# Three more output-projection steps by seven products, and another order of steps in the last three groups

## The chip, the core and the metric

The kernel runs on one core of a Trainium2 chip. The metric is the device time of one launch in microseconds; lower is better. The time before is 1044.01 us, the median of three runs that lie between 1043.68 and 1044.53.

## The reference, cut to what matters

One layer of a trunk: an RMS norm, a chunked gated linear attention with its output projection, a residual, another RMS norm and a squared-ReLU MLP, and a last RMS norm, for 256 tokens of width 2048 in float32. The change lives in the line of the output projection, `@ w_out`, a product of 256 x 2048 by 2048 x 2048.

```python
def _gla_mixer(h, w_in, w_gate_up, b_gate, o_norm, w_out):
    ...
    o = o.transpose(1, 0, 3, 2, 4).reshape(bsz, seq, GLA_VAL_WIDTH).astype(h.dtype)
    return (o * jax.nn.silu(r)) @ w_out
...
        h = h + _gla_mixer(_rmsnorm(h, gla_norm[j]), gla_w_in[j], gla_w_gate_up[j],
                           gla_b_gate[j], gla_o_norm[j], gla_w_out[j])
        h = h + _sq_relu_mlp(_rmsnorm(h, mlp_norm[i]), mlp_w_up[i], mlp_w_down[i])
    return _rmsnorm(h, final_norm)
```

## The kernel before

**Precision.** Every float32 operand is split into a rounded part (`hi`) and the rest (`lo`). A product is three matmuls: hi by hi, lo by hi, hi by lo. ScalarE makes `hi` by a copy (L118) and VectorE makes `lo` by a subtraction (L131, L165, L763). Split weights live in slots, `slots()`, five for `hi` and five for `lo`; a slot is free again when the last matmul that reads it is done. Raw weights come by DMA into six `raw` tiles.

**The stages.** The input projections come first, then attention, whose result `on` is gated; then the output projection (`out_group`, about 287 to 375 us), the up projection and the down projection of the MLP, and the last norm. TensorE's order is written out by hand: `then_mm` puts each block of matmuls behind the block before it. ScalarE's copies keep their order too (`copy_hi`). VectorE's order is less bound: each sum follows the split of its own step, and the split of the sums follows the split of the step after.

**A group and its steps.** The projection goes in four groups of 512 output columns. A group has eight steps, one for each pair `kp` of 128-row blocks of `w_out`, in an order given as a list. A step loads a 256 x 512 piece of weights. There are two ways to take it.

- A plain step: `lo` of all 1024 columns (two blocks of 512), and 24 matmuls of 256 columns.
- A step by sums: the 2 x 2 blocks of weights and activations are multiplied with seven products instead of eight, by sums and differences of blocks, 21 matmuls. One of the sums of weights is made by the DMA itself: the piece comes in two loads on the SP queue, and a third load on GpSimd's queue adds a block to one that has landed (L734). VectorE splits 768 columns (L131), makes two more sums in place (`weight_sums`, L597 and L598), and when ScalarE has copied those, splits them as well (1024 columns, L763, a second slot). This second half (`pending`) is multiplied behind the next step's products. Two PSUM banks hold sums over all the steps by sums of a group, `sums_banks`. When the last of these steps is done, ScalarE copies the two banks out (L769, L770), VectorE combines them (L771 to L774), and adds them to the group's two ordinary banks into `h` (L777).

The sums of activations, the *forms*, are made once, when `on` is transposed: `turn` transposes eight 128 x 128 blocks on TensorE (L620), and for a pair in `FORMED` calls `turn_pair`, which scales two blocks, makes the sums on VectorE (L610), and splits all eight blocks (L611 on ScalarE, L612 on VectorE). Other pairs get two plain scaled splits (L633 on ScalarE, L634 on VectorE for each of two row blocks).

**What goes on between steps.** `out_group` takes a table of calls to be made behind given steps. In the first group the last two turns of `on` stand behind the second step. In the other three, behind the second step stands the turn of the `h` of the group before (for the up projection), behind the fifth its squares (`ssq_h`, L782). Behind the fourth step `begin_out` copies the old `h` of the next group into its banks (L677).

The pairs by sums are 0, 1 and 7 in every group, so twelve steps of 32. Their order is 3, 0, 2, 1, 4, 7, 5, 6, in which the steps by sums are the second, the fourth and the sixth.

Of the kernel before, what the change touches and what calls it, by code (L numbers as in the profile page):

```python
# [33 lines left out]
T = 256  # L34
# [12 lines left out]
G = 1024  # L47
# [12 lines left out]
OFF = 48  # L60
# [8 lines left out]
def tile_gla_mlp(ctx, tc, x, xt, cols, w_vg, w_in, w_gate, w_out, w_up, w_down, final_norm, out):  # L69
# [19 lines left out]
    def aux_bank():  # L89
        aux_free.rotate(-1)  # L90
        return psum_bank(aux_free[-1], "aux")
# [151 lines left out]
    g2 = lambda kt: colt[:, KT + kt : KT + kt + 1]  # L243
# [88 lines left out]
    h = const.tile([P, NT, D], F32, name="h")  # L332
# [244 lines left out]
    oth = otl = None  # L577
# [13 lines left out]
    def form_sums(f, tt):  # L591
        tt(f[:, S3], f[:, A21], f[:, A11], ALU.subtract)
        tt(f[:, S2 : S1 + 1], f[:, A22 : A22 + 1].to_broadcast([P, 2, P]), f[:, 0::7], ALU.add)
        tt(f[:, S4], f[:, A12], f[:, S2], ALU.subtract)
# [2 lines left out]
        nc.vector.tensor_tensor(u[:, 2], u[:, 0], u[:, 2], op=ALU.subtract)  # L597
        return nc.vector.tensor_tensor(u[:, 1::2], u[:, 1::2], u[:, 2:3].to_broadcast([P, 2, T]), op=ALU.subtract)  # L598

    FORMED = (0, 1, 7)  # L600
    in_forms = lambda a: a.rearrange("p (f s) -> p f s", f=8)
    raw_forms = [in_forms(some[:, 4:6].rearrange("p a b -> p (a b)")), in_forms(mid.tile([P, G], F32, tag="db", name="form"))]

    def turn_pair(kp, bank, gain, to):

        raw_form = raw_forms[kp == 1]
        for i in range(2):
            s = bank[:, i * T : (i + 1) * T].rearrange("p (t s) -> p t s", t=NT)
            nc.scalar.activation(raw_form[:, A12 + 1 - i :: 2], s, AF.Copy, scale=gain(2 * kp + i))
        form_sums(raw_form, lambda o, x, y, op: nc.vector.tensor_tensor(o, x, y, op=op))  # L610
        nc.scalar.copy(to[0], raw_form)  # L611
        nc.vector.tensor_tensor(to[1], raw_form, to[0].bitcast(F32), op=ALU.subtract)  # L612

    def turn(src, row, gain, q, forms_of=None, banks=None):

        bs = banks or [aux_bank(), aux_bank()]
        for i in range(4):
            kt, b, o = 4 * q + i, bs[i // 2], i % 2 * T
            for t in range(NT):
                newest[0] = nc.tensor.matmul(  # L620
                    b[:, o + t * P : o + (t + 1) * P], src[:, t, kt * P : (kt + 1) * P], ident, is_transpose=True,
                    start=i % 2 == t == 0, stop=i % 2 == t == 1, skip_group_check=True,
                ).ins
        for kp in (2 * q, 2 * q + 1):
            if forms_of and kp in FORMED:
                turn_pair(kp, bs[kp - 2 * q], gain, forms_of(kp))
                continue
            for kt in (2 * kp, 2 * kp + 1):
                i = kt - 4 * q
                b, o = bs[i // 2], i % 2 * T  # L630
                s = b[:, o : o + T].rearrange("p (t s) -> p t s", t=NT)
                dh, dl = row(kt)
                nc.scalar.activation(dh, s, AF.Copy, scale=gain(kt))  # L633
                nc.vector.scalar_tensor_tensor(dl, s, gain(kt), dh.bitcast(F32), op0=ALU.mult, op1=ALU.subtract)  # L634
# [4 lines left out]
    oth, otl = (big.tile([P, KT * T + 192], F32R, tag="B", name="ot" + i) for i in "hl")  # L639
# [4 lines left out]
    def forms_o(kp):  # L644
        if kp < 2:
            return [of_pairs[:, kp, i] for i in range(2)]
        return [a[:, OFF : OFF + G].rearrange("p (f s) -> p f s", f=8) for a in (oth, otl)]

    def place_o(kt):

# [5 lines left out]
    def row_o(kt, t):  # L656
        if kt // 2 in FORMED:
            return [a[:, (A11, A21)[t] - kt % 2] for a in forms_o(kt // 2)]
        o, d = place_o(kt)
        return [a[:, o + t * d : o + t * d + P] for a in (oth, otl)]  # L660
# [12 lines left out]
    def begin_out(g):  # L673

        for t in range(NT):
            out_banks[g, t] = bank = psum_bank(out_ids[2 * (g % 2) + t])
            nc.scalar.copy(bank, h[:, t, g * GT : (g + 1) * GT])  # L677

    def spare_out(g):
        return [psum_bank(out_ids[2 * (1 - g % 2) + t], "aux") for t in range(NT)]  # L680

    side.extend([nothing, lambda: turn(on, turned_o, gain_o, 0, forms_o)])
    side.extend([nothing, lambda: turn(on, turned_o, gain_o, 1, forms_o)])
    side.extend([nothing] * 6 + [lambda: begin_out(0)])
    r_banks = list(acc_free)
# [93 lines left out]
    def ssq_h(g):  # L779
        for t in range(NT):  # L780
            sq = tmp.tile([P, GT], F32, tag="t512", name="sq", bufs=1)
            nc.scalar.activation(sq, h[:, t, g * GT : (g + 1) * GT], AF.Square, accum_out=hs[:, t, g : g + 1])  # L782

    ORDER = (3, 0, 2, 1, 4, 7, 5, 6)
    newest[0] = None
    ordered[0] = True
    out_group(0, ORDER, FORMED, {
        1: lambda: (turn(on, turned_o, gain_o, 2), turn(on, turned_o, gain_o, 3, forms_o, spare_out(0))),
        3: lambda: begin_out(1),
    })  # L790
    hth, htl = (big.tile([P, KT, T], F32R, tag="A" + i, name="h" + i, bufs=1) for i in "hl")
    turned_h = lambda kt: [a[:, kt, :].rearrange("p (t s) -> p t s", t=NT) for a in (hth, htl)]
    for g in range(1, GROUPS):
        out_group(g, ORDER, FORMED, {
            1: lambda: turn(h, turned_h, g2, g - 1), 4: lambda: ssq_h(g - 1),
            **({3: lambda: begin_out(g + 1)} if g + 1 < GROUPS else {}),
        })
    sums = [big.tile([P, 4, T], F32, tag="E" + i, name="sums", bufs=1) for i in "hl"]
# [444 lines left out]
    for t in range(NT):  # L1243
# [19 lines left out]
        for on_act, lo, hi in ((0, 0, 256), (1, 1280, 1536), (0, 256, 768), (1, 1536, 2048), (0, 768, 1280)):  # L1263
            s = hf[:, t, lo:hi]
# [44 lines left out]
```

## Time and profile before

| | |
|---|---|
| median of the runs | 1044.01 us |
| the profiled execution | 1044.42 us |
| its span, first to last instruction | 1042.4 us |
| TensorE matmuls | 9058, busy 99% of the span |
| VectorE | 865.6 us busy, 83% |
| ScalarE | 737.1 us busy, 71% |
| GpSimd | 119.8 us busy, 11% |
| DMA | 226.79 MB, mean 218 GB/s |
| granted TensorE clock | 0.998 of full speed |

In the views, PE is TensorE, PEld its weight loads, DVE VectorE, ACT ScalarE, POOL GpSimd, and SPq the queue that issues most loads. `L715` is line 715 of the kernel: all matmuls of the output projection. A row of a timeline gives the start and the duration in us, the engine, the line, what it writes and reads by the program's names, how many instructions are merged, and in brackets how long the engine stood idle before it and what ended the wait. A merged row's duration runs from the first start to the last end, and instructions of one engine overlap a little, so the cost of one is read from start to start.

### The profile page before, as it was taken

Reading aid. Unit: us, or ns where it says so; the run is one execution under the profiler, and the core shown is the slowest. Engines: PE = TensorE matmul, PEld = TensorE weight load, DVE = VectorE, ACT = ScalarE, POOL = GpSimd, SP = SyncE. Lnnn points to the kernel's source line nnn. Section 1 sums busy time; section 2 is a strip of 40 time slices with the busy share of each in tenths; the row PEclk is TensorE's granted clock in tenths of the full one; section 3 lists DMA queues with packets and bytes.
Section 4 is the critical chain, followed back from the end, with each engine's and each line's share of the span. In section 5 each row is a group of like instructions: output and inputs, shape, how many; then the busy total and the mean of one; then the engine's idle time right before and its main releaser. Section 6 shows DMA issues by size and latency. Waiting matters only on the chain.

```text
span 1042.4 us, 23169 instructions
## 1 busy us (share of the span) xinstructions
PE 1034.2 (99%) x9058; PEld 1033.3 (99%) x9058; DVE 865.6 (83%) x1171; ACT 737.1 (71%) x1088; POOL 119.8 (11%) x163
## 2 busy tenths in 40 slices
PE   9999999999999999999999999999999999999997
PEld 9999999999999999999999999999999999999997
DVE  5768654656499876889999999999999999999887
ACT  6785544546477764677788788778778778878685
POOL 0000000010111101111111111111111111211100
PEclk9999999999999999999999999999999999999999
DMA  9957665555667786678887888887888888887772
GB/s 339 333 170 212 194 198 165 157 148 182 184 188 206 214 260 194 175 213 227 232 236 230 242 229 225 233 240 219 243 236 224 248 228 229 234 232 220 233 242 90
DMA packets 118733, 226.79 MB, mean 218 GB/s; under 512 B 10672, under 2 KB 27184, under 8 KB 118496
## 3 DMA queue, kind: packets, MB, share of 16 engines
q1 hardware_dynamic: 100096, 207.39, 63.3%
q0 software_dynamic: 17856, 16.26, 10.3%
q8 instruction: 71, 1.16, 0.4%
q10 hardware_dynamic: 672, 1.66, 0.4%
q14 instruction: 38, 0.31, 0.1%
HBM read 223.17 MB, written 2.10 MB: 216 GB/s over the span
## 4 chain that ended last, share of the span: by engine, by line
PE 96%; DMA 2%; issue 1%; ACT 0%; DVE 0%; SPq 0%; POOLq 0%; POOL 0%; DVEq 0%; ACTq 0%
PE up L857 33%; PE acc L857 28%; PE acc L176 17%; PE acc L715 8%; PE acc L219 6%; PE aux L219 2%; DMA raw<-in_w_vg 2%; PE aux L176 1%; PE aux L620 1%; PE aux L521 1%; DVE lo L131 0%; ACT hi L118 0%; ACT sqf L1196 0%; SPq L168 0%; PE acc L422 0%
## 5 line engine op out<-in xcount | busy, mean ns | idle before, releaser
L118 ACT CAST hi<-raw 128x512 fp32r<-128x512 f32 (+4 forms) x634 | 512.1, 834 | 231.5 <-PE acc L176 64.3
L131 DVE TENSOR_TENSOR lo<-raw,hi 128x768 fp32r<-128x768 f32 (+3 forms) x226 | 238.1, 1057 | 95.9 <-ACT hi L118 93.2
L857 PE MATMUL acc<-hi,act 128*128 128x256 f32 x1696 | 247.7, 276 | 0.0
L857 PE MATMUL up<-hh,hi 128*128 128x256 f32 x1024 | 238.7, 276 | 0.0
L857 PE MATMUL up<-hl,hi 128*128 128x256 f32 x1024 | 238.7, 276 | 0.0
L165 DVE TENSOR_TENSOR lo<-raw,hi 128x1024 fp32r<-128x1024 f32 x160 | 194.8, 1220 | 28.2 <-ACT hi L118 26.2
L857 PEld LDWEIGHTS acc<-hi,act 128*128 128x128 f32 x1696 | 217.6, 188 | 0.0
L857 PEld LDWEIGHTS up<-hh,hi 128*128 128x128 f32 x1024 | 192.3, 188 | 0.0
L857 PEld LDWEIGHTS up<-hl,hi 128*128 128x128 f32 x1024 | 192.3, 188 | 0.0
L1067 POOL DMA_DIRECT2D raw<-in_w_down x112 | 97.4, 869 | 516.9 <-DMA raw<-in_w_down 245.5
L1127 DVE TENSOR_TENSOR lo<-raw,hi 128x1024 fp32r<-128x1024 f32 x112 | 136.4, 1218 | 1.1 <-ACT hi L118 1.1
L857 PE MATMUL up<-hh,lo 128*128 128x256 f32 x1024 | 137.0, 276 | 0.0
L857 PE MATMUL acc<-lo,act 128*128 128x256 f32 x848 | 133.8, 276 | 0.0
L857 PEld LDWEIGHTS up<-hh,lo 128*128 128x128 f32 x1024 | 125.7, 188 | 0.0
L857 PEld LDWEIGHTS acc<-lo,act 128*128 128x128 f32 x848 | 113.3, 188 | 0.0
L176 PE MATMUL acc<-hi,xA 128*128 128x256 f32 (+1 forms) x728 | 105.2, 278 | 0.0
L176 PEld LDWEIGHTS acc<-hi,xA 128*128 128x128 f32 x728 | 93.5, 188 | 0.5 <-ACT hi L118 0.5
L598 DVE TENSOR_TENSOR raw<-raw 128x512 f32<-128x512 f32 x124 | 85.6, 691 | 3.2
L176 PE MATMUL acc<-lo,xA 128*128 128x256 f32 (+1 forms) x364 | 60.8, 278 | 0.1
L597 DVE TENSOR_TENSOR raw<-raw 128x256 f32<-128x256 f32 x124 | 52.4, 423 | 2.9
L176 PEld LDWEIGHTS acc<-lo,xA 128*128 128x128 f32 x364 | 50.3, 188 | 0.3 <-DVE lo L131 0.3
L219 PE MATMUL acc<-xA,hi 128*128 128x256 f32 x288 | 49.2, 276 | 0.0
(181 smaller groups left out, 1225.9 us busy)
## 6 DMA issues: line engine op xcount, KB each, us to landing
raw<-in_w_up SPq DMA_DIRECT2D x128, 512.0 KB, 4.5
raw<-in_w_down SPq DMA_DIRECT2D x224, 256.0 KB, 4.5
raw<-in_w_in SPq DMA_DIRECT2D x80, 512.0 KB, 3.7
raw<-in_w_down POOLq DMA_DIRECT2D x112, 128.0 KB, 5.2
raw<-in_w_out SPq DMA_DIRECT2D x20, 512.0 KB, 4.5
raw<-in_w_down SPq DMA_DIRECT2D x16, 512.0 KB, 4.9
raw<-in_w_vg SPq DMA_DIRECT2D x14, 520.0 KB, 8.4
raw<-in_w_out SPq DMA_DIRECT2D x24, 256.0 KB, 3.7
```

Source lines behind the costliest of these rows:

```text
L118: last_hi[0] = nc.scalar.copy(to, raw)
L131: last_lo[0] = nc.vector.tensor_tensor(lo[:, s], raw[:, s], hi[:, s].bitcast(F32), op=ALU.subtract)
L165: last_lo[0] = nc.vector.tensor_tensor(to[1], dst, to[0].bitcast(F32), op=ALU.subtract)
L176: nc.tensor.matmul(o[:, m], x, w[:, m], start=first and c == 0, stop=last, skip_group_check=True)
L219: nc.tensor.matmul(o, u[:, i, s], m, start=kt == 0 and n == 0 and j % 2 == 0, stop=kt == KT - 1 and n == 2, skip_group_check=True,)
L521: nc.tensor.matmul(o, kab[:, k[0], c0 + c, k[1] : k[1] + P], q(qt[:, c0 + c]), start=c == 0, stop=c == 1)
L597: nc.vector.tensor_tensor(u[:, 2], u[:, 0], u[:, 2], op=ALU.subtract)
L598: return nc.vector.tensor_tensor(u[:, 1::2], u[:, 1::2], u[:, 2:3].to_broadcast([P, 2, T]), op=ALU.subtract)
L715: newest[0] = nc.tensor.matmul(bank[:, o + d : o + d + T], x, w[:, d : d + T], start=bank in sums_banks and bank.name not in begun, stop=l ...
L857: newest[0] = nc.tensor.matmul(o, x, w, start=first, stop=last, skip_group_check=True).ins
L1067: nc.gpsimd.dma_start(out=raw[:, :T], in_=src[:, 0, T:], accum_op=ALU.add)
L1127: last_lo[0] = nc.vector.tensor_tensor(to[1][:, :G], u, to[0][:, :G].bitcast(F32), op=ALU.subtract)
```

## The change

Pair 6 gets forms, so that pairs 0, 1, 6 and 7 can be taken by sums. The forms lie in the place of pairs 6 and 7 of the transposed `on` (those of 7 stay in the place of pairs 0 and 1). The first group keeps its order and its three steps by sums. In the other three groups four steps go by sums, which makes 3 + 3 x 4 = 15, and the order is 0, 3, 1, 4, 7, 2, 6, 5: the steps by sums are the first, third, fifth and seventh, and alternate with the plain ones. The second half of the seventh step, with the copies and combinations that follow it, thus comes behind the products of the last step of the group. The turn of the `h` of the group before moves from behind the second step to behind the fifth, its squares from behind the fifth to behind the seventh. `begin_out` stays behind the fourth.

```diff
-    FORMED = (0, 1, 7)
+    FORMED = (0, 1, 6, 7)
...
-        raw_form = raw_forms[kp == 1]
+        raw_form = raw_forms[kp % 2]
...
     def forms_o(kp):
         if kp < 2:
             return [of_pairs[:, kp, i] for i in range(2)]
-        return [a[:, OFF : OFF + G].rearrange("p (f s) -> p f s", f=8) for a in (oth, otl)]
+        c = (12 * T + OFF + 128, OFF)[kp - 6]
+        return [in_forms(a[:, c : c + G]) for a in (oth, otl)]
...
-    ORDER = (3, 0, 2, 1, 4, 7, 5, 6)
     newest[0] = None
     ordered[0] = True
-    out_group(0, ORDER, FORMED, {
+    out_group(0, (3, 0, 2, 1, 4, 7, 5, 6), (0, 1, 7), {
...
     for g in range(1, GROUPS):
-        out_group(g, ORDER, FORMED, {
-            1: lambda: turn(h, turned_h, g2, g - 1), 4: lambda: ssq_h(g - 1),
+        out_group(g, (0, 3, 1, 4, 7, 2, 6, 5), FORMED, {
+            4: lambda: turn(h, turned_h, g2, g - 1), 6: lambda: ssq_h(g - 1),
             **({3: lambda: begin_out(g + 1)} if g + 1 < GROUPS else {}),
         })
```

## The prediction

> **What bounds the kernel now.** I read the page first, its busy line and its chain, and then asked for the busy time in each stage of the output projection, because an average over 1042 us says nothing of a change that lives in 88 us. In the first fence the reader is to see that TensorE is never free and that the chain that ended last is TensorE's own work.
>
> ```profile
> PE 1034.2 (99%) x9058; PEld 1033.3 (99%) x9058; DVE 865.6 (83%) x1171; ACT 737.1 (71%) x1088; POOL 119.8 (11%) x163
> ...
> PE 96%; DMA 2%; issue 1%; ACT 0%; DVE 0%; SPq 0%; POOLq 0%; POOL 0%; DVEq 0%; ACTq 0%
> ```
>
> The second view cuts the projection at the transposes of each group; one row is a stretch, TensorE's busy time, its weight loads, VectorE's, ScalarE's and GpSimd's, then clock, DMA share and GB/s.
>
> ```profile
> 285.30:313.97 28.67, 28.67 (x256) 28.67 (x255) 26.22 (x39) 22.91 (x37) 2.62 (x3) 1.00 0.63 181
> 313.97:335.66 21.69, 21.69 (x194) 21.69 (x192) 20.16 (x29) 16.01 (x28) 2.65 (x3) 1.00 0.75 220
> 335.66:357.40 21.74, 21.74 (x194) 21.74 (x193) 19.56 (x28) 15.20 (x27) 2.62 (x3) 1.00 0.76 225
> ```
>
> TensorE stands still in none of them, at full granted clock, so time is lost or won there matmul by matmul. But VectorE, 83% busy over the span, is 93% and 90% busy in these two groups. It is the engine with the least left, and the change gives it more work.
>
> **The change part by part. TensorE's gain.** A plain step multiplies 24 times (four pairs of token tile and row block, six each), a step by sums 21 times (seven products of three). The timeline of TensorE gives the price of one:
>
> ```profile
> 312.94 0.84 PE L715 MATMUL acc<-hi,of 128*128 128x256 f32 x6
> 313.62 0.51 PE L715 MATMUL acc<-lo,of 128*128 128x256 f32 x3
> 313.97 1.04 PE L620 MATMUL aux<-ident,h 128*128 128x128 f32 x8
> ```
>
> Nine matmuls start 312.94 and the next thing starts 313.97, so one costs 0.114 us (six of them 0.68). Three steps more by sums save nine matmuls, 1.02 us in all, 0.34 in each of the last three groups: a group, cut at its transposes, goes from the 21.69 us of the second stretch above to 21.35. The transposes (eight, moved behind the fifth step) cost TensorE the same wherever they stand.
>
> **VectorE's price.** This is its timeline at the turn from the second to the third group (start, duration, and in brackets the idle time before):
>
> ```profile
> 331.30 0.42 DVE L771 TENSOR_TENSOR some<-some 128x256 f32<-128x256 f32 x1
> ...
> 332.84 0.68 DVE L777 TENSOR_TENSOR h<-acc,some 128x512 f32<-128x512 f32 x1
> 333.44 0.95 DVE L131 TENSOR_TENSOR lo<-raw,hi 128x768 fp32r<-128x768 f32 x1
> 334.30 0.68 DVE L777 TENSOR_TENSOR h<-acc,some 128x512 f32<-128x512 f32 x1
> 334.90 0.41 DVE L597 TENSOR_TENSOR raw<-raw 128x256 f32<-128x256 f32 x1
> 335.35 0.69 DVE L598 TENSOR_TENSOR raw<-raw 128x512 f32<-128x512 f32 x1
> 335.96 1.22 DVE L131 TENSOR_TENSOR lo<-raw,hi 128x1024 fp32r<-128x1024 f32 x1
> 337.29 1.23 DVE L763 TENSOR_TENSOR lo<-raw,hi 128x1024 fp32r<-128x1024 f32 x1
> 338.44 0.87 DVE L634 SCALAR_TENSOR_TENSOR hl<-aux,colt,hh 128x256 fp32r<-128x256 f32 x2
> ...
> 344.45 1.23 DVE L763 TENSOR_TENSOR lo<-raw,hi 128x1024 fp32r<-128x1024 f32 x1 [0.69 <-ACT hi L118]
> ...
> 350.63 1.23 DVE L131 TENSOR_TENSOR lo<-raw,hi 128x1024 fp32r<-128x1024 f32 x1 [0.62 <-PE acc L715]
> ```
>
> From start to start, a step by sums costs 0.86 (L131, 768 wide: 333.44 to 334.30) + 0.45 (L597 to L598) + 0.61 (L598 to the next) + 1.15 (L763: 337.29 to 338.44) = 3.07 us; a plain step only one 1024-wide split, 1.15. The end of a group is 1.54 for the four combinations (331.30 to 332.84) and twice 0.60 for h, 2.74; a turn is four L634, 1.74. Before, a group is 3 x 3.07 + 5 x 1.15 + 2.74 + 1.74 = 19.44, which the stage's 19.56 confirms. After, it is 4 x 3.07 + 4 x 1.15 + 4.48 = 21.36 us, against TensorE's 21.35. The two engines are level, if VectorE never waits.
>
> It does wait. In the stretch of 21.74 us it is idle 2.18; 0.62 of that is at 350.63, where it waited for TensorE to free a slot (it was ahead, which costs nothing); the other 1.56 are waits in its own work, the largest the 0.69 at 344.45, where the second split of a step by sums (L763) waits for ScalarE's copies of the sums, which wait for the sums. One of three steps by sums shows that wait there, so a fourth adds a third of 0.69: 1.79 us a group. What excess there is goes first against VectorE's lead, the stock of split weights in the five slots:
>
> ```profile
> 303.58 3.22 DVE L131 TENSOR_TENSOR lo<-raw,hi 128x1024 fp32r<-128x1024 f32 x3
> ...
> 307.95 0.39 PE L715 MATMUL acc<-lo,oth 128*128 128x256 f32 x2
> ```
>
> The first of those three splits (ending at 304.80, one duration of 1.22 on) belongs to the last step of the first group, and TensorE first uses it at 307.95: a lead of 3.15 us. The forms of pair 6 take from it. In the first group's turn two L634 (0.80) give way to three sums and a 1024-wide split like these rows of another pair:
>
> ```profile
> 294.40 0.28 DVE L610 TENSOR_TENSOR some<-some 128x128 f32<-128x128 f32 x1
> ...
> 295.87 0.42 DVE L610 TENSOR_TENSOR some<-some 128x256 f32<-128x256 f32 x1
> ...
> 299.93 1.22 DVE L612 TENSOR_TENSOR otl<-some,oth 128x1024 fp32r<-128x1024 f32 x1
> ```
>
> That is 0.28 + 0.42 + 0.28 + 1.22 less the overlap of some 0.3, 1.9, so 1.1 more; a 1024-wide ScalarE copy of about 1 us beside it is hidden in ScalarE's 5.8 idle us of that stage, and at worst it delays the split by that 1 us. Lead left: about 2.0 us.
>
> The sum: three groups x 1.79 = 5.4, less 2.0 of lead, is 3.4 us in which TensorE waits; less the 1.02 gained, +2.4. Ends: if every wait but one 0.69 in a group is filled, 3 x 0.7 - 2.0 = 0.1 and the change gains 0.9; if the fourth sums step's wait comes in full on top of 1.79, 3 x 2.48 - 2.0 = 5.4 and it loses 4.4. I take the middle, since it is nearest to the stage's own measured idle. The lead may be empty when the up projection begins; the same engine has 15.82 busy of 24.60 there in before, so nothing is carried on:
>
> ```profile
> 375.40:400.00 24.60, 24.60 (x219) 24.60 (x218) 15.82 (x24) 13.31 (x19) 1.08 (x2) 1.00 0.73 231
> ```
>
> **What the new order does at a group's end.** Before, the last sums pair is finished ahead of a plain step, so the combinations run under 24 matmuls with stock in the slots. Now it is the last work of its group. Two ScalarE copies must empty the two sums banks, and the next group, which opens by sums, writes one of them at once.
>
> ```profile
> 330.03 0.58 ACT L769 COPY some<-acc 128x512 f32<-128x512 f32 x1
> 330.51 0.59 ACT L770 COPY some<-acc 128x512 f32<-128x512 f32 x1
> ```
>
> The first copy takes 0.58; six of the nine opening matmuls use another bank and cover 0.68 of it. Taken as 0; at most a weight copy stands ahead of it on ScalarE (0.83, the 339.48 row below), 0.83 + 0.58 - 0.68 = 0.73 at each of two boundaries, 1.5; at best nothing, since no row lets a bank come free earlier.
>
> **Loads, turns and copies.** A step by sums has two loads on SP for one and one accumulating load on GpSimd: three more issues on each queue (0.89 each on GpSimd's, which is busy 2.6 of 21.7 us). The tightest pair of before:
>
> ```profile
> 331.24 0.89 POOL L734 DMA_DIRECT2D raw<-in_w_out x1 [4.02 <-DMA raw<-in_w_out]
> ...
> raw<-in_w_out POOLq DMA_DIRECT2D x9, 128.0 KB, 5.4
> ...
> 339.48 0.83 ACT L118 CAST hi<-raw 128x768 fp32r<-128x768 f32 x1
> ```
>
> 331.24 + 5.4 is 336.6, and the copy starts at 339.48: 2.8 us to spare, with DMA at 0.76. Taken as 0; a late raw tile of a slow VectorE could eat the 2.8. The turn moved from the second to the fifth step stands 99 matmuls, 11.3 us, into the group, and reads an h that is now finished about 4 us into it (two copies, 1.1; the combinations and h, 2.74): 0. The copies of `begin_out`, which wait for that h on ScalarE, have weight copies queued behind them; TensorE needs their banks only a group later and those copies are split into slots ahead of use: 0, with the same 0.83 of one weight copy as the upper end. The squares on ScalarE, moved too, have 5 us of idle time in the group: 0.
>
> A rule that speaks otherwise: the trace has weight loads busy 99% and TensorE idle nowhere in these stages. The Trainium skill, Trainium Kernel Development and Optimization, section Performance Expectations, has the distance to the roof judged by MFU and by LDWEIGHTS busy. By it TensorE alone is the limit and the sum would be the nine matmuls, -1.0; by the stage rows of VectorE it is +2.4. I go by the rows, because a level second engine has to come first.
>
> **The rivals.**
> - Not slower: VectorE's order fills its waits and five slots carry it. For it: before shows no TensorE wait with 19.44 of work. Against: 21.36 + 0.7 is above 21.35 already. It decides when VectorE's own waits stay under about 0.7 us a group. 1044.42 - 0.9 = 1043.5 on the profiled execution.
> - Boundary and loads on top: the bank copies queue behind a weight copy (1.5), or a sums pair lands late. For it: ScalarE's copies are issued in a fixed order; against: 2.8 us of room in the loads. 1044.42 + 2.4 + 1.5 = 1048.3.
> - The lead holds nothing, waits at the upper end: 1044.42 + 4.4 = 1048.8, one with the second for the chances.
>
> **How the numbers follow.** The profiled execution took 1044.42, 0.41 above the median of the runs shown (1044.01). The forecast, 1044.42 + 2.4 less 0.41, is 1046.4. Chances: VectorE bound 0.57 (its own range 1044.0 to 1048.0), cover holds 0.30, the heavy case 0.13. The range must hold the cover case (1043.1 against the median) and most of the heavy one: 1043.0 to 1048.8. A measurement tells about 0.2%, 2.1 us, from no change. Slower by more: 0.13 and six tenths of 0.57, 0.48. Faster by more needs twice the nine matmuls: 0.03. Within: 0.49.
>
> **What would show it.** 723 matmuls of L715 for 732 (15 x 21 + 17 x 24 for 12 x 21 + 20 x 24), and 15 accumulating loads for 12. Step 1 (gain): the three last groups' matmul time down 0.34 each. Step 2 (price): VectorE at 97% and over between groups, and TensorE gaps that end with VectorE's splits, mostly in the plain steps of the third and fourth group, while "ACT hi waits for PE acc" nearly goes. If the gaps end with ScalarE's L769 and L770, the boundary rival is right; if with an accumulating load, the loads are. No gaps at all and 1043.1 would say that the waits I counted can be filled. I would be wrong altogether if gaps appear after the projection, in stages that the change does not touch.

## The result and the profile after

The changed kernel takes 1049.77 us (median of six runs, 1048.01 to 1051.24) against 1044.11 for the kernel before (1043.68 to 1044.53): a ratio of 1.0051, 95% interval 1.0041 to 1.0061. By the medians it is slower by 5.7 us (5.3 by the ratio), where 2.4 were forecast, and it lies above the range of the forecast. The profiled execution took 1049.81.

The busy line and the chain of the changed kernel's page, the same two lines as those quoted for the kernel before:

```profile
PE 1037.4 (99%) x9049; PEld 1035.5 (99%) x9049; DVE 871.5 (83%) x1182; ACT 738.1 (70%) x1095; POOL 122.4 (12%) x166
...
PE 92%; issue 3%; DMA 2%; DVE 1%; ACT 0%; SPq 0%; POOL 0%; POOLq 0%; DVEq 0%; ACTq 0%
```

Nine matmuls fewer, as they should be, and yet TensorE is busy 3.2 us longer. Busy time can grow with fewer matmuls only when they start further apart: a wait shorter than a matmul's recorded 0.28 us does not show as idle time. The stages say where (stretch, then busy TensorE, weight loads, VectorE, ScalarE, GpSimd, clock, DMA share, GB/s):

```profile
313.97:335.66 21.69, 21.69 (x194) 21.69 (x193) 18.81 (x28) 16.19 (x28) 2.65 (x3) 1.00 0.73 205
335.66:357.40 21.74, 21.68 (x185) 21.09 (x184) 20.35 (x31) 15.66 (x29) 3.50 (x4) 1.00 0.77 213
357.40:400.00 42.60, 40.53 (x331) 39.65 (x331) 34.14 (x47) 25.70 (x41) 1.96 (x3) 0.96 0.73 234
...
385.00:390.00 5.00, 3.21 (x29) 3.01 (x27) 3.35 (x6) 2.20 (x5) 0.85 (x2) 1.00 1.02 385
390.00:395.00 5.00, 4.82 (x26) 4.69 (x27) 1.68 (x5) 2.61 (x5) 0.23 (x1) 0.66 0.34 114
```

The last two rows lie in the up projection, 10 us and more behind the stage that was changed: TensorE idle for 1.8 us, and then 26 matmuls in 5 us at a mean granted clock of 0.66. The waits of the changed kernel's TensorE, over the whole span, are two that show as idle time, and the second is the one at the very start that the kernel before has too:

```profile
PE row L820 <- DVE work L812: 2.0, 1, 2.0
PE aux L252 <- DVE ones L249: 1.1, 1, 1.1
```

L820 is a matmul of the diagonals of the second norm's factors, in `last_turn`, early in the up projection.

To part the loss I compared the start times of all TensorE matmuls of both traces. Against before, the projection (first matmul of the projection to the first of the up projection) is 1.07 us longer, 88.72 for 87.65. The up projection loses 2.13 us up to L820 and 2.2 more in the next 100 matmuls, 4.34 together. The start of the projection is 0.11 earlier. 1.07 + 4.34 - 0.11 is 5.30 us, and from there on every matmul stands 5.30 us later than before, to the last one. The two spans differ by 5.64; the other 0.34 lies behind the last matmul, where the runs below differ by -0.05 to 0.66 us, and was not followed up.

**The up projection.** VectorE, changed kernel, end of the last group:

```profile
374.80 5.76 DVE L165 TENSOR_TENSOR lo<-raw,hi 128x1024 fp32r<-128x1024 f32 x5
380.48 0.42 DVE L772 TENSOR_TENSOR some<-some 128x256 f32<-128x256 f32 x1
380.81 1.22 DVE L165 TENSOR_TENSOR lo<-raw,hi 128x1024 fp32r<-128x1024 f32 x1
...
385.94 0.68 DVE L778 TENSOR_TENSOR h<-acc,some 128x512 f32<-128x512 f32 x1
...
390.26 0.29 DVE L812 TENSOR_SCALAR work<-ident,r 128x128 f32<-128x128 f32 x1 [0.23 <-POOL r L356]
```

The same operations before the change:

```profile
374.60 0.41 DVE L771 TENSOR_TENSOR some<-some 128x256 f32<-128x256 f32 x1
...
377.87 0.68 DVE L777 TENSOR_TENSOR h<-acc,some 128x512 f32<-128x512 f32 x1
...
382.26 0.28 DVE L812 TENSOR_SCALAR work<-ident,r 128x128 f32<-128x128 f32 x1
```

And TensorE there, changed kernel first, then before:

```profile
387.94 0.28 PE L857 MATMUL up<-hl,hi 128*128 128x256 f32 x1
390.18 0.92 PE L820 MATMUL row<-work,ones 128*128 128x128 f32 x4 [1.97 <-DVE work L812]
390.93 1.40 PE L620 MATMUL aux<-ident,h 128*128 128x128 f32 x8
...
392.56 0.41 PE L857 MATMUL up<-hh,hi 128*128 128x256 f32 x1
392.77 0.41 PE L857 MATMUL up<-hl,hi 128*128 128x256 f32 x1
```

```profile
386.97 0.28 PE L857 MATMUL up<-hl,hi 128*128 128x256 f32 x1
387.09 0.60 PE L820 MATMUL row<-work,ones 128*128 128x128 f32 x4
387.53 1.04 PE L620 MATMUL aux<-ident,h 128*128 128x128 f32 x8
```

Five splits of up weights stand ahead of the first combination now. ScalarE is late as well. Its copies of the two sums banks, which the combinations read, stand behind a row of weight copies and start 2.0 us after the first up matmul (376.26); before, they started 2.0 us ahead of it (373.28 for 375.30). First the changed kernel, then before:

```profile
373.00 5.37 ACT L118 CAST hi<-raw 128x512 fp32r<-128x512 f32 x6 [0.21 <-DVE raw L598]
378.27 0.57 ACT L770 COPY some<-acc 128x512 f32<-128x512 f32 x1
378.75 0.58 ACT L771 COPY some<-acc 128x512 f32<-128x512 f32 x1
```

```profile
373.28 0.58 ACT L769 COPY some<-acc 128x512 f32<-128x512 f32 x1
```

The last h is written 8.1 us later than before (385.94 for 377.87), the diagonals 8.0 us later, and TensorE, for which they were 4.5 us early, waits two. Then its matmuls start 0.21 us apart for 0.113, at half clock.

**The projection.** VectorE and TensorE of the changed kernel at the start of the third group:

```profile
334.89 1.22 DVE L764 TENSOR_TENSOR lo<-raw,hi 128x1024 fp32r<-128x1024 f32 x1
336.02 0.69 DVE L778 TENSOR_TENSOR h<-acc,some 128x512 f32<-128x512 f32 x1
336.62 2.08 DVE L131 TENSOR_TENSOR lo<-raw,hi 128x768 fp32r<-128x768 f32 x2
```

```profile
336.16 0.74 PE L716 MATMUL acc<-lo,of 128*128 128x256 f32 x4
336.74 0.86 PE L716 MATMUL acc<-hi,of 128*128 128x256 f32 x6
337.63 0.62 PE L716 MATMUL acc<-lo,of 128*128 128x256 f32 x3
```

The split that starts at 336.62 ends at 337.57 (0.95, the 768-wide one of the quoted rows), and the matmuls that need it start at 337.63: no lead is left. Seven such waits of 0.05 to 0.23 us stand in the third and the fourth group, all but one in their first 8 us, and none in the second. Behind each of them the next start is late too, by 0.11 us. These long starts sum to 1.82 us, and 0.25 more comes from matmuls at a slower pace, below: 2.07, less the 1.02 gained, is 1.05 of the 1.07.

### The profile page after: what moved, and what is told of

Read it like the earlier page. It is cut to its first block, busy times and chain, and to the rows that moved or that the text cites. A ratio compares the mean times of both kernels' runs of the same rounds, so it can differ in the third digit from the quotient of the medians.

```text
span 1048.0 us, 23174 instructions
## 1 busy us (share of the span) xinstructions
PE 1037.4 (99%) x9049; PEld 1035.5 (99%) x9049; DVE 871.5 (83%) x1182; ACT 738.1 (70%) x1095; POOL 122.4 (12%) x166
## 4 chain that ended last, share of the span: by engine, by line
PE 92%; issue 3%; DMA 2%; DVE 1%; ACT 0%; SPq 0%; POOL 0%; POOLq 0%; DVEq 0%; ACTq 0%
PE up L857 32%; PE acc L857 28%; PE acc L176 17%; PE acc L219 6%; PE acc L716 5%; PE aux L219 2%; DMA raw<-in_w_vg 2%; PE aux L176 1%; PE aux L521 1%; PE aux L620 1%; DVE lo L131 1%; DMA raw<-in_w_out 1%; ACT hi L118 0%; ACT sqf L1196 0%; SPq L168 0%
## 5 line engine op out<-in xcount | busy, mean ns | idle before, releaser
L598 DVE TENSOR_TENSOR raw<-raw 128x512 f32<-128x512 f32 x127 | 87.7, 690 | 3.2
```

## The experiments

All times are device time beside runs of the kernel before on the same chip (medians of 1044.1 to 1044.4). The table gives, from the start times of TensorE's matmuls in each run's trace, how much longer the projection and the up projection are than before, and when the last group's first combination starts and its h ends, counted from the first up matmul.

| kernel | steps by sums | median us | ratio (95%) | projection | up projection | first combination | h done |
|---|---|---|---|---|---|---|---|
| before | 12 | | | 0 | 0 | -0.7 | 3.2 |
| changed | 15 | 1049.77 | 1.0051 (1.0041 to 1.0061) | +1.07 | +4.34 | 4.2 | 10.4 |
| last group old | 14 | 1046.46 | 1.0018 (1.0009 to 1.0028) | +1.81 | 0.00 | 0.2 | 6.1 |
| last turn later | 15 | 1046.75 | 1.0039 (1.0016 to 1.0061) | +1.09 | | 4.2 | 10.4 |
| wait filled | 15 | 1048.05 | 1.0037 (1.0023 to 1.0052) | +1.07 | +2.44 | 4.2 | 10.4 |
| h first | 15 | 1046.79 | 1.0023 (1.0014 to 1.0033) | +1.09 | +1.11 | 2.0 | 4.8 |
| order alone | 12 | 1044.32 | 1.0001 (0.9992 to 1.0011) | 0.00 | 0.00 | -0.8 | 4.5 |
| only last group new | 13 | 1044.83 | 1.0005 (0.9996 to 1.0015) | -0.34 | +0.83 | 2.0 | 7.7 |
| side by side | 15 | 1046.26 | 1.0018 (1.0008 to 1.0027) | +1.19 | +0.46 | -0.9 | 3.1 |
| h first, turn later | 15 | 1046.13 | 1.0017 (1.0007 to 1.0027) | +1.07 | +0.51 | 1.9 | 4.8 |
| last two swapped | 15 | 1046.77 | 1.0024 (1.0014 to 1.0033) | +2.27 | 0.00 | 1.5 | 6.6 |
| spread | 15 | 1046.86 | 1.0024 (1.0014 to 1.0033) | +0.81 | +1.21 | 0.2 | 5.3 |
| thirteen, h first | 13 | 1043.80 | 0.9995 (0.9985 to 1.0004) | -0.34 | 0.00 | 0.6 | 3.4 |
| fourteen | 14 | 1045.64 | 1.0013 (1.0004 to 1.0023) | +0.07 | +1.11 | 1.9 | 4.8 |

Two theories went in: that the loss is one late h behind the projection (L), and my prediction's, that VectorE is over-full in three groups (V).

**The last group put back.** Groups 2 and 3 keep the change.

```diff
+        new = g < GROUPS - 1
-        out_group(g, (0, 3, 1, 4, 7, 2, 6, 5), FORMED, {
-            4: lambda: turn(h, turned_h, g2, g - 1), 6: lambda: ssq_h(g - 1),
+        out_group(g, (0, 3, 1, 4, 7, 2, 6, 5) if new else (3, 0, 2, 1, 4, 7, 5, 6), FORMED if new else (0, 1, 7), {
+            4 if new else 1: lambda: turn(h, turned_h, g2, g - 1), 6 if new else 4: lambda: ssq_h(g - 1),
```

> The last group gets back its old order, its three steps by sums and its old places of turn and squares; groups 2 and 3 keep the change (14 steps by sums). Theory L (late h): 4.8 of the 5.6 us lost between the two profiled executions lie at one place behind the projection, where TensorE waits 2.1 us for the row of norm factors and then runs at half clock, because the last group's combinations came late; with them under the last step again this goes, and the time is about 1044.5 us (1043.8 to 1045.2). Theory V (my prediction, VectorE over-full in three groups): a third of the loss goes, about 1048 us.

The up projection loses nothing, as L says. But the projection is longer than the change's, and the total lies between the two theories. Its waits name a new place: the turn, back behind the second step, now stands in front of an h that the group before finishes late.

```profile
PE aux L620 <- DVE h L778: 1.0, 2, 0.9
```

So the turn's move was needed in a group that follows one ending with a sums pair.

**The last turn later.**

```diff
-    side.extend([nothing] * 3 + [scale2, nothing, scale2_diagonals] + [nothing] * 2 + [last_turn])
+    side.extend([nothing] * 3 + [scale2, nothing, scale2_diagonals] + [nothing] * 4 + [last_turn])
```

> The changed kernel with the last turn and the row of norm factors two half-steps (2.7 us of matmuls) later in TensorE's order. Theory L: the wait of 2.1 us is covered, the clock stays at 1.00 and the time is about 1045.7 us (up to 1046.7 if the turn's splits are then late for the last pairs). Theory V: no change, about 1049.8. If the fall of the clock has another cause than the wait: about 1047.7.

Moving nothing but TensorE's request for the row takes 3 us off, 1046.75: most of the up projection's loss is that wait and what it draws after it. Eight of this kernel's ten runs lie between 1046.5 and 1047.1, two at 1055.4 and 1055.8, and the profiled execution is one of these two; so only its projection stands in the table. Its trace has the row wait 0.5 us and no low clock, and then, from 394 to 622 us, 1939 matmul starts in a row that are 118 ns apart instead of 113, at a granted clock of 1.00. That is 8.7 us, the slower pace of the last section.

```profile
400.00:600.00 200.00, 200.00 (x1700) 200.00 (x1699) 174.95 (x228) 144.25 (x207) 31.23 (x36) 1.00 0.77 212
```

In the same 200 us the kernel before has 1767 matmuls for these 1700.

**The wait filled with matmuls.**

```diff
         with then_mm():
+            for _ in range(8):
+                newest[0] = nc.tensor.matmul(b[:, :P], ones, ones, start=True, stop=True).ins
+        with then_mm():
```

> The changed kernel with eight more 128x128 matmuls of ones, whose result is overwritten, ahead of the row of norm factors: two rows of the same kind took 0.44 us, so eight are 1.8 us inside the wait of 2.1. If the idle time itself halves the clock: the wait stays, the clock keeps 1.00, and about 2 us go, 1047.8. If the clock falls for another reason: no change, 1049.8. If the wait is not idle time of TensorE's but order: 1051.6.

The row comes about as late as in the change (2.04 us for 2.13), but the granted clock stays at full in the whole stage and 1.7 us of time go:

```profile
376.40:400.00 23.60, 23.48 (x205) 23.09 (x204) 16.98 (x25) 13.68 (x21) 1.08 (x2) 1.00 0.78 271
```

That is the price of the half clock and of what follows it, and the half clock is shown here to follow from the idle time: the data and their lateness are the same. (In the traces 1.9 us go, and 0.3 of them are the slower pace of the last section, which the change has in 91 starts behind its low clock and this run in 23.)

**The last h first.** ScalarE's copies and VectorE's splits from the fourth up pair on are put behind the last group's.

```diff
+            if n_raw[0] is not None and n_raw[0] > 3:
+                order.enter_context(tc.issue_after(last_comb[0].ins))
...
+                    if n_raw[0] is not None and n_raw[0] > 3:
+                        order.enter_context(tc.issue_after(last_h[0].ins))
...
+                        last_comb[0] = nc.scalar.copy(comb[:, 0:4:3], two(p57))
...
+            last_h[0] = tt(o, two(banks[t]), comb[:, 4 * t : 4 * t + 2], op=ALU.add)
```

> The changed kernel with an order written out: ScalarE copies the last group's two sums banks, and VectorE makes the four combinations and h, ahead of the fourth split of up-projection weights and all behind it. Theory L: h is done about 4 us earlier, the row is there before TensorE asks, no low clock; what is left is the projection's own +0.8, so about 1045.0 us (1044.5 to 1045.8). Theory V: no change, 1049.8. If VectorE has no room there: the up projection waits for its fourth or fifth split and the time lies between, 1046 to 1048.

h is done 5.6 us earlier and the clock stays up. Yet a wait of 0.9 us is left at the row, and the time is 1.8 us above what I expected:

```profile
PE row L824 <- DVE work L816: 0.9, 1, 0.9
```

The splits that were held back now stand ahead of the small operations behind h. An order written out in one place moved the queue to the next.

**The order alone**, with pair 6 plain.

```diff
-    FORMED = (0, 1, 6, 7)
+    FORMED = (0, 1, 7)
```

> Only the order and the later turns and squares; pair 6 stays plain, so twelve steps by sums (first, third and fifth of each of the last three groups). Its last sums are multiplied with two plain steps still to come. If the loss is that the last sums pair ends its group (late h, and combinations against the next group's splits): no wait, 1044.4 us (within 0.6 of before). If the order or the moved turn costs by itself: projection more than 1 us longer, over 1045.4.

Nothing is lost, to the hundredth, in both stages. The order of pairs and the late turns cost nothing by themselves, with twelve steps by sums.

**Only the last group new.**

```diff
+        new = g == GROUPS - 1
-        out_group(g, (0, 3, 1, 4, 7, 2, 6, 5), FORMED, {
+        out_group(g, (0, 3, 1, 4, 7, 2, 6, 5) if new else (3, 0, 2, 1, 4, 7, 5, 6), FORMED if new else (0, 1, 7), {
...
```

> Only the last group in the new order with four steps by sums, groups 2 and 3 as before: thirteen steps by sums, one group end with the sums pair last, and it is the one in front of the up projection. Late h: the whole 4.3 us of the up projection stays (wait of 2.1 us and the low clock), the projection gains 0.3 and may lose as much: about 1048.5 us. VectorE over-full in three groups: a third of the loss, about 1046.

L's number was wrong by 3.7 us and V's by 1.2. The projection gains its 0.34, with no wait at all. At the row stands a wait of 0.56 and no low clock:

```profile
387.71 0.49 PE L821 MATMUL row<-work,ones 128*128 128x128 f32 x2 [0.56 <-DVE work L813]
```

A sums pair at the end of the last group is thus worth 0.8 us. The rest of the 4.3 comes only with the groups before it changed too: the first combination starts 4.2 us behind the first up matmul with three such groups, 2.0 with one. Of these 2.2 us, 1.3 stand already in ScalarE's queue, whose copies of the sums banks start 2.0 us behind that matmul with three and 0.7 with one. L and V are both needed, and what arrives late from the groups before is ScalarE as well as VectorE; how much of the one follows from the other isn't shown.

**Neighbouring sums, and two more orders with the same work on VectorE.**

```diff
-        out_group(g, (0, 3, 1, 4, 7, 2, 6, 5), FORMED, {
-            4: lambda: turn(h, turned_h, g2, g - 1), 6: lambda: ssq_h(g - 1),
+        out_group(g, (0, 1, 3, 4, 7, 6, 2, 5), FORMED, {
+            2: lambda: turn(h, turned_h, g2, g - 1), 4: lambda: ssq_h(g - 1),
```

> Fifteen steps by sums as in the change, but in the order 0, 1, 3, 4, 7, 6, 2, 5: the steps by sums in neighbouring twos (first and second, fifth and sixth), two plain steps at the end of the group, the turn behind the third step and the squares behind the fifth. VectorE's work is the same. If the group's end is the cause: combinations fall under plain steps, h is early, no waits, and the nine matmuls show: 1043.4 us. If VectorE's sum of 21.36 us against 21.35 is the cause: waits of 2 us or more stay in the projection, over 1045.5.

Swapped last two, the turn as in the change:

```diff
-        out_group(g, (0, 3, 1, 4, 7, 2, 6, 5), FORMED, {
+        out_group(g, (0, 3, 1, 4, 7, 6, 2, 5), FORMED, {
```

> The changed kernel with the last two pairs 6 and 5 brought one forward and 2 put back: order 0, 3, 1, 4, 7, 6, 2, 5 in the last three groups, fifteen steps by sums, the last of them sixth instead of seventh, turn and squares as in the change. If the damage is done by the sums pair that ends its group: combinations under the last plain step, h about 2.7 us earlier, the row waits at most 0.5 us and the clock stays; projection +0.5 or less; 1044.4 to 1045.2. If VectorE's amount of work does it: projection +1 and a late h as in the change, 1048 or more.

Spread, the turn as in the change:

```diff
-        out_group(g, (0, 3, 1, 4, 7, 2, 6, 5), FORMED, {
+        out_group(g, (3, 0, 1, 4, 7, 6, 2, 5) if g == 1 else (0, 3, 4, 1, 7, 6, 2, 5), FORMED, {
```

> Fifteen steps by sums, group 2 in the order 3, 0, 1, 4, 7, 6, 2, 5 and groups 3 and 4 in 0, 3, 4, 1, 7, 6, 2, 5: a plain step stands between the first group's end and the first two sums, two plain steps of three close each group, turn behind the fifth step. VectorE's work is that of the change. If placement is all: no wait, -1.0 against before, 1043.3 us. If VectorE's 21.36 us a group do not fit 21.35 of TensorE: waits again, 1045 or more.

All three end with plain steps, and in none is the last h as late as in the change or the clock halved. But all three lose time in the projection, 0.8 to 2.3 us, and so none of the two answers is right. "Swapped" has real waits in it, up to 0.7 us each, and 2.4 us in all with the late starts behind them. The longest are at the split of the sums: two steps by sums stand side by side there, with the turn between them. "Side by side" has one wait, 0.5 us, in the second group. "Spread" has no wait in the projection, and one of 0.5 us at the row; what it loses in the projection is another thing:

```profile
340.09 0.87 PE L716 MATMUL acc<-hi,of 128*128 128x256 f32 x6
340.80 0.52 PE L716 MATMUL acc<-lo,of 128*128 128x256 f32 x3
341.15 0.28 PE L716 MATMUL acc<-hi,oth 128*128 128x256 f32 x1
```

Nine matmuls here take 1.06 us, 118 ns each, where nine of the same kind in the kernel before took 1.03 (the rows quoted from 312.94), 114 ns, at the same granted clock. Counted over the projection and the first 100 matmuls of the up projection, 551 starts of "spread" are 116 to 150 ns apart, and cost 2.6 us over the normal pace; 500 in "side by side" (2.3 us), 105 in the change (0.55), 48 in the kernel before (0.30, the eleven or twelve behind each turn).

**Two combinations of the parts.** The edit of "h first", and the last turn one place later:

```diff
-    side.extend([nothing] * 3 + [scale2, nothing, scale2_diagonals] + [nothing] * 2 + [last_turn])
+    side.extend([nothing] * 3 + [scale2, nothing, scale2_diagonals] + [nothing] * 3 + [last_turn])
```

> The changed kernel with the combinations and h written ahead of the fourth up split and with the last turn one half-step (1.36 us of matmuls) later. The first alone left a wait of 1.0 us at the row; now it should be covered, so that the up projection loses nothing (at most 0.4 at the turn's own splits) and the projection's +1.1 is what is left: 1045.5 us (1045.3 to 1046.0). If a wait goes over into the turn's splits: 1046.5.

The wait is covered, and the forecast of what is left (+1.07) is right, but 0.5 more is lost in the up projection at the slow pace, and 1046.13 lies just above the range expected. And thirteen steps, the edit of "only the last group new" with that of "h first":

```diff
+            if n_raw[0] is not None and n_raw[0] > 3:
+                order.enter_context(tc.issue_after(last_comb[0].ins))
...
+        new = g == GROUPS - 1
-        out_group(g, (0, 3, 1, 4, 7, 2, 6, 5), FORMED, {
+        out_group(g, (0, 3, 1, 4, 7, 2, 6, 5) if new else (3, 0, 2, 1, 4, 7, 5, 6), FORMED if new else (0, 1, 7), {
...
```

> Thirteen steps by sums (only the last group in the new order, which alone left the projection 0.34 us shorter and a wait of 0.7 us at the row), with the last group's combinations and h written ahead of the fourth up split. If that wait is the late h alone: it goes, and 0.3 us less than before, 1044.0. If the h cannot come earlier because the sums pair ends the group: 0.5 us of it stays, 1044.5.

This is the version that the parts point to: the projection 0.34 shorter, no wait, h at 3.4 us, 1043.80 us. In its trace it beats the kernel before by what three matmuls are worth; in run time the interval (0.9985 to 1.0004) doesn't tell it from no change.

**Fourteen**, with a plain step first in the group behind the first sums end, and the edit of "h first":

```diff
+        new = g % 2
+        out_group(g, (0, 3, 1, 4, 7, 2, 6, 5) if new else (3, 0, 2, 1, 4, 7, 5, 6), FORMED if new else (0, 1, 7), {
             4: lambda: turn(h, turned_h, g2, g - 1), 6: lambda: ssq_h(g - 1),
```

> Fourteen steps by sums: groups 2 and 4 in the new order with four, group 3 in the old order with three, the turns behind the fifth step in all three, and the last group's combinations and h written ahead of the fourth up split. The group that follows a sums pair at a group's end opens with a plain step now. If it is two such ends in a row, with a sums step behind each, that makes VectorE late: no wait anywhere, six matmuls fewer, -0.7 us against before, about 1043.6. If one end in the middle is enough: +0.5 to +1 in the projection, 1044.4 or more.

There is no wait in the projection. That does not make two such ends in a row the cause: in the changed kernel the third group already waits, and only one sums pair at a group's end, that of the second group, stands ahead of it. In the change and in "last group old" the waits at a group's start come where a step by sums opens the group behind such an end; here a plain step opens it, and there are none. But that group also has one step by sums fewer here, and which of the two takes the waits away isn't separated. 215 starts at the slow pace (1.1 us) eat the six matmuls, and the row waits 0.9 us again, as in "h first".

## Why the prediction was wrong

- **The gain** was right: 9049 matmuls, and 0.34 us for the group that "only last group new" changes, seen alone.
- **VectorE's price** had the mechanism and the wrong size. Forecast: 3.4 us of TensorE waits in three groups. Measured: 2.07 with the slow pace, for a net +1.07 instead of +2.4. The excess was read as steady (1.79 us a group); the waits sit in the third and fourth group, nearly all at their starts, where the combinations and h of the group before stand among the splits. With the last sums earlier and spread out, the same 21.36 us of work gave no projection wait, though TensorE's group then took 22.1 us at its slow pace, so that it fits into 21.35 isn't shown. The sum for a group before, 19.44, met the 19.56 of the third group; that the same view has 20.16 for the second was left aside. Of the signs, ScalarE's waits for TensorE to free a slot did nearly go (11.8 us in ten waits before, 1.0 in one after). VectorE at 97% did not come: between the turns of the second, third and fourth group it is busy 87% and 96%. "Mostly in plain steps" was wrong too: five of the seven waits stand in steps by sums.
- **The step that failed** is "The lead may be empty when the up projection begins ... so nothing is carried on". I asked only whether VectorE has room in the up projection for its splits. The work carried over was not splits of that stage but the last group's copies and combinations, behind which hangs a chain (h, its squares, the norm's factors, their diagonals) that TensorE asks for at a fixed place, 11.8 us into the up projection. That term was put at 0 and measured 4.34: 2.13 of waiting at the row, and 2.2 behind it, at half clock for the most part. The closing sentence, gaps in a stage that the change does not touch, names the case that came.
- **The boundary rival** (ScalarE's copies of the sums banks late for the next group) did not happen between the groups. No TensorE wait in the trace ends with those copies; at the three ends that a group follows they wait for TensorE themselves:

```profile
ACT some L770 <- PE acc L716: 2.9, 3, 1.1
```

At the end of the last group, which the prediction did not look at for this, the copies did queue: they start 2.0 us behind the first up matmul, behind a row of weight copies, and are a part of the late h.

- **Loads**: no TensorE wait ends with one. The fifteen accumulating loads fit.
- **The rule on weight loads** of the Trainium skill (Trainium Kernel Development and Optimization, Performance Expectations), which I set against the rows, would have given -1.0. LDWEIGHTS are 99% busy in the change too, and more than 5 us were lost.

The direction was right, and the waits in the projection that were given as its reason are a fifth of the loss.

## What to carry to other kernels

Ask of a change in one stage not only what it adds there, but which of its results is used at a fixed place behind it, and how early that result is now; here it was 4.5 us early, and the rows that show it were not looked at. When an engine is nearly full, where a chain stands in its queue can count for more than the sum of its work: the seven kernels with fifteen steps by sums and no added matmuls lie between 1046.1 and 1049.8 us. A wait of two microseconds on TensorE can cost four, so a late request is cheaper than an early one.

## What was not expected of the hardware

- **A short wait halves the clock.** TensorE is idle for 2.0 us (2.24 from start to start), matmuls run again for 1.3 us, and then the granted clock falls to 0.50. In one-microsecond stretches of the changed kernel:

```profile
389.50:390.50 1.00, 0.32 (x2) 0.30 (x2) 0.52 (x2) 0.00 (x0) 0.73 (x2) 1.00 0.82 223
390.50:391.50 1.00, 1.00 (x10) 0.90 (x9) 0.05 (x1) 0.37 (x1) 0.00 (x0) 0.98 0.88 315
391.50:392.50 1.00, 1.00 (x7) 1.00 (x6) 0.42 (x1) 0.61 (x3) 0.00 (x0) 0.50 0.40 152
...
394.50:395.50 1.00, 1.00 (x9) 1.00 (x9) 0.00 (x0) 0.99 (x2) 0.00 (x0) 0.82 0.00 0
```

It lasts 3.4 us, and a wait of 0.9 us ("h first", "fourteen") does not bring it on. The Trainium skill, TensorE: Matmul & The Clock Gate, Part 1, has the clock fall after an idle window of about 3.4 us and come back after a busy one. The length of the slow time agrees; the idle time that was enough is shorter here, 2.0 us, and the measurement decides.

- **A slower pace without a lower clock.** After turns, and behind some short waits, TensorE's matmuls start 118 ns apart instead of 113 at a granted clock of 1.00. In the kernel before it ends after eleven or twelve. In "spread" it holds from each turn to the next, and from the last to the row. In two of the ten runs of "last turn later" the time is 9 us longer, and the trace of one of them has the pace for 1939 matmuls; so it need not come out the same in two runs of one kernel, and a trace tells the pace of its own execution only. Why it starts and what ends it stays open: no run here changed it by itself. In the projection it cost up to 2.6 us, and there 8.7, more than the change could gain.
